# Entry of the second layer in a two-layer Mamba-2/MLA step: the last row square and the scaling of the third row group moved behind columns of the first group, gate weight remainders computed in four parts

## Chip, cores and metric

The kernel runs on one core of a Trainium2 chip. The metric is the device time in microseconds (us) of one execution. The profile is of one execution on the same kind of core.

## What is computed

One inference step of a two-layer decoder trunk. Layer 0 is a Mamba-2 mixer, layer 1 multi-head latent attention (MLA) with a gate. There are 1024 prompt tokens and 64 sample tokens (8 requests of 8), 1088 rows of width 1024, all in fp32. The part that matters here, cut from the reference, is the seam between the two layers:

```python
hp = hp + out_p                        # residual rows after layer 0 (hs likewise)
ln = rms_norm(hp, norm_w[1])           # x * rsqrt(mean(x*x) + 1e-6) * w
proj = einsum('btd,de->bte', ln, w_in) # layer 1: 512 query, 256 latent, 32 rope, 1024 gate columns
gate = proj[..., o3:]                  # later: o * silu(gate)
```

## The kernel before

**Precision.** Matmuls run on rounded fp32 operands. Each operand is held as two tiles, a rounded `h` part and the remainder `l` = x - h, and a product is three matmuls: h*h, l*h, h*l. So the normalised, transposed activations are `hh` and `hl`, and a weight block has `wgh` and `wgl` (gate) or `ck0h`/`ck0l` and so on (latent and rope columns). `split` (L127) makes such a pair: ACT copies to `h`, and another engine subtracts for `l`; for the gate and latent weights that is POOL (`eng=k.nc.gpsimd`).

**End of layer 0.** `ssd_out` (L792) finishes the residual rows in 9 tiles: rows 0 to 7 of 128 tokens, row 8 of 64. For each row and each half of 512 columns, PE makes a projection `pob` in PSUM and DVE adds it to the residual row `xrb` (L808). Row 8 needs a second add per half (L810), since its products lie in two halves of the PSUM tile. Then the row goes to DRAM (L815; rows 7 and 8 by POOL's queue), ACT squares it with a running sum (L818), DVE and POOL make of the sum the row's factor `hrs` (`rstd_of`, L202 and L207), and for rows 0 to 5 DVE multiplies the row by it at once (`scale_row`, L213) into `xt`.

**Entry of layer 1.** `norm_steps(..., tail=True)` (L258, called from `mla_in` at L967) takes the rows in three groups: rows 0 to 2, 3 to 5, 6 to 8 (384, 384 and 320 tokens). It first scales rows 6 to 8 (L260 to L262). Then `norm_cols` (L242) goes through the 8 column blocks of 128 of each group: PE transposes the block's three row pieces into a PSUM tile `xtp` (L248, three transposes), ACT writes `hh` of it (L250), DVE writes `hl` (L251). There are three `xtp` buffers, so the fourth block's transposes need the first block's `hl` done. I write T0,0 to T2,7 for the transposes by group and block.

After each group, `proj_piece` of the first two gate blocks (`gate_block`, L920) uses these columns: per block and gate three matmuls of 384 (or 320) columns, L88, into PSUM tiles `pj`. There are two `pj` buffers, which the projections `pob` of layer 0 used just before. A scheduler mixes all of this: each engine has one queue, run in order, and the scheduler chooses the order within it from the dependencies and its own estimates; `issue_after` holds an instruction behind a named one. A gate block ends with ACT's Silu out of PSUM (L925) and a DMA. Gate blocks 2 to 7 follow (`mla_in`, L972 to L980), then the latent, query and attention stages.

**Loads.** `load_w` (L283) puts each weight block's DMA on SP's queue (L285) into raw buffers, two for the gate blocks and two for the `ck` blocks. A third block's DMA therefore waits until POOL has made the first block's remainder, and SP's queue is in order too.

Of the kernel before, what the change touches and what calls it, by code (L numbers as in the profile page):

```python
# [8 lines left out]
F32 = mybir.dt.float32  # L9
# [7 lines left out]
D = 1024  # L17
# [106 lines left out]
    pass  # L124


def split(k, hi, lo, src, eng=None):  # L127
    nc = k.nc
    nc.scalar.copy(hi, src)  # L129
    (eng or nc.vector).tensor_tensor(lo, src, hi.bitcast(F32), op=ALU.subtract)  # L130


def setup(k, stack):
# [73 lines left out]
    nc.gpsimd.tensor_tensor(out, out, e, op=ALU.pow)  # L207


def scale_row(k, i, pool):  # L210
    xr, m = k.hr[i]
    xt = pool.tile([128, D], F32, tag="xt", name=f"xt{i}", bufs=3 if i > 5 else 6)
    k.nc.vector.tensor_scalar(xt[:m], xr[:m], k.hrs[:m, i : i + 1], None, op0=ALU.mult)  # L213
    return xt, m, 128 * (i % 3)
# [27 lines left out]
def norm_cols(k, gi, xs, wcol, hi, lo, psum):  # L242
    nc = k.nc
    t0, n = TG[gi]
    for d in range(8):
        p = psum.tile([128, 512], F32, tag="tr", name=f"xtp{gi}_{d}", bufs=PB["tr"])
        for xt, m, o in xs:
            nc.tensor.transpose(p[:, o : o + m], xt[:m, d * 128 : d * 128 + 128], k.ident[:m, :m])  # L248
        k.cols[gi].append(
            nc.scalar.activation(hi[:, d, t0 : t0 + n], p[:, :n], AF.Copy, scale=wcol[:, d : d + 1]))  # L250
        nc.vector.scalar_tensor_tensor(  # L251
            lo[:, d, t0 : t0 + n], p[:, :n], wcol[:, d : d + 1], hi[:, d, t0 : t0 + n].bitcast(F32),
            op0=ALU.mult, op1=ALU.subtract)
    if gi == 2:
        nc.gpsimd.tensor_copy(hi[:, :, T:], lo[:, :, SEQ:].bitcast(F32))


def norm_steps(k, load, wcol, hi, lo, pool, psum, steps, xbufs, before=None, after=None, tail=False):  # L258
    if tail:
        for i in range(6, 9):  # L260
            k.hrows.append(scale_row(k, i, pool))
    rows = k.hrows[:3] if tail else norm_rows(k, 0, load, pool, xbufs)  # L262
    if before is not None:
        before()
        wcol = k.normc[0]
    k.cols = [[], [], []]
    for gi in range(3):
        norm_cols(k, gi, rows, wcol, hi, lo, psum)
        if gi < 2:
            rows = k.hrows[3 * gi + 3 : 3 * gi + 6] if tail else norm_rows(k, gi + 1, load, pool, xbufs)  # L270
        if after is not None and gi == 0:
            after()
        for st in steps:
            next(st)


def load_raw(pool, nk, ncol, bufs=2):
# [2 lines left out]
    return t.rearrange("p (k e) -> p k e", k=nk)  # L280


def load_w(k, pool, src, nk, ncol, tag, bufs=3, raws=None, rbufs=2, eng=None):  # L283
    raw = load_raw(raws or pool, nk, ncol, rbufs)
    k.nc.sync.dma_start(raw, src.rearrange("(k p) e -> p k e", p=128))  # L285
    hi = pool.tile([128, nk, ncol], F32R, tag=tag + "h", name=tag + "h", bufs=bufs)
    lo = pool.tile([128, nk, ncol], F32R, tag=tag + "l", name=tag + "l", bufs=bufs)
    split(k, hi, lo, raw, eng)
    return hi, lo


# [501 lines left out]
def ssd_out(k, items, ypools, psum):  # L793
# [3 lines left out]
    for n, (ph, i) in enumerate(items):  # L797
# [3 lines left out]
        for hf in range(2):  # L801
# [9 lines left out]
            if hf == 0:  # L811
                if n + 1 < len(items):
                    nxt = items[n + 1][0].prep(items[n + 1][1], ypools[(n + 1) % 2], psum)
                yield
        (nc.gpsimd if ph.k0 and i > 6 else nc.sync).dma_start(k.h_d[t0 : t0 + m], xr[:m])  # L815
        if ph.k0:
            sq = k.tok.rearrange("p i a h -> p (i a h)")[:, :D]
            nc.scalar.activation(sq[:m], xr[:m], AF.Square, accum_out=k.hssq[:m, i : i + 1])  # L818
            rstd_of(k, k.hrs[:m, i : i + 1], k.hssq[:m, i : i + 1], D)
            k.hr.append((xr, m))  # L820
            if i < 6:
                k.hrows.append(scale_row(k, i, k.h0p))
        yield
# [94 lines left out]


def gate_block(k, wp, raws, b):  # L920
    ws = kslices(load_w(k, wp, k.I["mla_w_in"][0][:, 800 + 128 * b : 928 + 128 * b], 8, 128, "wg", 3, raws, eng=k.nc.gpsimd), 8)
    gt = wp.tile([128, T], F32, tag="gt", name=f"gt{b}", bufs=2)

    def ev(ci, t0, n, p):
# [1061 lines left out]
```

## Time and profile before

| | us |
|---|---|
| median of 3 runs | 1981.43 (1976.2, 1981.67, 1981.43) |
| the profiled execution, its own time | 1988.45 |
| its span, first to last instruction | 1986.7 |
| PE busy in the span | 1909.0 (96%) |
| DVE, ACT, POOL busy | 1204.0, 1110.3, 837.9 |
| 1054.61 to 1096.50 (entry of layer 1): length, PE busy, mean TensorE clock | 41.89, 37.31, 0.92 |
| 1096.50 to 1172.50 (gate blocks 2 to 7): the same | 76.00, 75.00, 1.00 |

How to read it. Times in the rows are from the span's start. A row of the timeline merges neighbours of one kind on one engine: start, length, engine, line, output <- input, shape, count, and in brackets how long the engine sat idle before and what ended that. A row of the windows view gives for a stretch the busy time of each engine with its count of instructions, then the clock granted to TensorE (1.00 is full), the mean busy share of the DMA engines, and GB/s. "PEld" is the weight load that goes along with each matmul. Buffer numbers are left out in the profile's names, and kept in the rows of order below.

### The profile page before, as it was taken

How to read it: one execution, taken by the hardware profiler on the slowest of the kernel's cores; microseconds unless marked ns; L12 is line 12 of the kernel's file. 1: busy time of each engine (PE TensorE's matmuls, PEld its weight loads, DVE VectorE, ACT ScalarE, POOL GpSimd, SP SyncE). 2: the span in 40 equal slices, each digit the busy share in tenths (PEclk: the TensorE clock that was granted, in tenths of full speed). 3: DMA queues.
4: the chain of work that ended last, by engine and by line, in shares of the span. 5: the costliest groups of instructions: out<-in, count | busy, mean ns of one | idle time of the engine just before them, and what ended most of it. 6: DMA issues, size and time to landing. Idle time of an engine off the chain costs nothing. (4 is left out here: it accounts for less than half of the span.)

```text
span 1986.7 us, 33396 instructions
## 1 busy us (share of the span) xinstructions
PE 1909.0 (96%) x12001; PEld 1738.7 (88%) x12001; DVE 1204.0 (61%) x2439; ACT 1110.3 (56%) x2535; POOL 837.9 (42%) x1018
## 2 busy tenths in 40 slices
PE   6999999999999999899999999998999999899998
PEld 5999999999999999788787998997888887688887
DVE  4557575756665656755434114566788787766665
ACT  5456666666666666633214224436777777645552
POOL 1537455555655555443003221204333335755541
PEclk9999999999999999999999999999999999899999
DMA  4223323332333332645433242222111113544441
GB/s 152 59 65 88 90 84 96 83 106 83 95 83 95 81 96 89 200 153 183 148 126 121 89 165 66 99 84 74 45 50 40 50 40 100 189 139 140 138 146 38
DMA packets 181228, 202.12 MB, mean 102 GB/s; under 512 B 18844, under 2 KB 147752, under 8 KB 180680
## 3 DMA queue, kind: packets, MB, share of 16 engines
q1 hardware_dynamic: 176008, 180.21, 29.9%
q0 software_dynamic: 4976, 19.66, 3.1%
q8 instruction: 95, 1.56, 0.3%
q14 instruction: 69, 0.57, 0.1%
q10 hardware_dynamic: 80, 0.13, 0.0%
HBM read 146.65 MB, written 53.28 MB: 101 GB/s over the span
## 5 line engine op out<-in xcount | busy, mean ns | idle before, releaser
L88 PE MATMUL pj<-xh,wih 128*128 128x384 f32 (+1 forms) x768 | 255.8, 337 | 5.0 <-ACT xh L250 4.4
L88 PE MATMUL pj<-xl,wih 128*128 128x384 f32 (+1 forms) x768 | 255.3, 332 | 0.6 <-DVE xl L251 0.6
L88 PE MATMUL pj<-xh,wil 128*128 128x384 f32 (+1 forms) x768 | 254.6, 332 | 0.0
L1344 POOL TENSOR_TENSOR tl<-P,th 128x384 fp32r<-128x384 f32 (+1 forms) x96 | 91.9, 957 | 160.8 <-ACT P L1342 119.2
L487 DVE SCALAR_TENSOR_TENSOR acc<-raw,vec,acc 128x1112 f32<-128x1112 f32 x96 | 141.6, 1476 | 25.8 <-ACT acc L483 24.9
L88 PEld LDWEIGHTS pj<-xh,wih 128*128 128x128 f32 x768 | 145.1, 190 | 6.8 <-ACT xh L250 5.1
L88 PEld LDWEIGHTS pj<-xl,wih 128*128 128x128 f32 x768 | 145.7, 190 | 1.9 <-DVE xl L251 0.9
L88 PEld LDWEIGHTS pj<-xh,wil 128*128 128x128 f32 x768 | 145.5, 189 | 0.4
L100 PE MATMUL pz<-wih,xh 128*128 128x256 f32 x504 | 142.8, 287 | 0.8 <-ACT z L528 0.8
L100 PE MATMUL pz<-wil,xh 128*128 128x256 f32 (+1 forms) x504 | 140.2, 284 | 0.0
L1341 ACT ACTIVATE th<-st 128x512 fp32r<-128x512 f32 x192 | 94.5, 492 | 75.7 <-PE st L1337 54.9
L591 ACT ACTIVATE M<-M,tok 128x128 f32<-128x128 f32 (+1 forms) x288 | 90.9, 386 | 68.6 <-DVE M L588 68.4
L100 PE MATMUL pz<-wih,xl 128*128 128x256 f32 x448 | 128.3, 286 | 0.0
L1633 POOL TENSOR_TENSOR kvl<-pgr,kvh 128x1024 fp32r<-128x1024 f32 x32 | 77.6, 2424 | 71.6 <-ACT kvh L1632 71.6
L100 PEld LDWEIGHTS pz<-wih,xh 128*128 128x128 f32 x504 | 96.0, 190 | 1.6 <-ACT z L528 1.2
L588 DVE TENSOR_TENSOR M<-M,negu 128x512 f32<-128x512 f32 x64 | 52.2, 815 | 69.0 <-DMA M<-acs_d 68.7
L1342 ACT ACTIVATE P<-st 128x512 f32<-128x512 f32 x192 | 93.4, 486 | 0.0
L100 PEld LDWEIGHTS pz<-wil,xh 128*128 128x128 f32 (+1 forms) x504 | 92.7, 184 | 0.7
L130 DVE TENSOR_TENSOR wil<-wraw,wih 128x512 fp32r<-128x512 f32 x88 | 71.2, 815 | 30.4 <-ACT wih L129 27.1
L1344 DVE TENSOR_TENSOR tl<-P,th 128x512 fp32r<-128x512 f32 x96 | 74.8, 779 | 21.8 <-ACT P L1342 21.3
L574 POOL TENSOR_TENSOR xdd<-xsT,tok 128x256 f32<-128x256 f32 x64 | 51.2, 800 | 81.3 <-ACT xsT L560 81.0
L100 PEld LDWEIGHTS pz<-wih,xl 128*128 128x128 f32 x448 | 85.3, 190 | 0.1
(827 smaller groups left out, 6343.5 us busy)
## 6 DMA issues: line engine op xcount, KB each, us to landing
wraw<-in_ssd_w_in SPq DMA_DIRECT2D x92, 256.0 KB
M<-acs_d SPq DMA_DIRECT2D x64, 256.0 KB
s<-in_state_ssm SPq DMA_DIRECT2D x32, 256.0 KB
y_d<-y SPq DMA_DIRECT2D x64, 128.0 KB
out_s_ssm<-s SPq DMA_DIRECT2D x32, 256.0 KB
wraw<-in_ssd_w_out SPq DMA_DIRECT2D x12, 512.0 KB
q_d<-qt SPq DMA_DIRECT2D x32, 192.0 KB
qp<-q_d SPq DMA_DIRECT2D x8, 768.0 KB
```

The lines of the kernel that those rows point to most:

```text
L88: nc.tensor.matmul(out, a, b, start=(i == 0), stop=(i == n - 1))
L100: nc.tensor.matmul(o, a, b, start=(j == 0), stop=(j == len(ops) - 1))
L130: (eng or nc.vector).tensor_tensor(lo, src, hi.bitcast(F32), op=ALU.subtract)
L487: last = nc.vector.scalar_tensor_tensor(acc, raw[:, j : j + n], k.convw[j][:, blk : blk + 1], acc, op0=ALU.mult, op1=ALU.add)
L574: nc.gpsimd.tensor_tensor(v3(xdd), v3(xsT), hb(2), op=ALU.mult)
L588: nc.vector.tensor_tensor(M[:m, :, :m], M[:m, :, :m], (k.negs if smp else k.negu)[:m, :m].unsqueeze(1).to_broadcast([m, 4, m]), op=ALU.add)
L591: nc.scalar.activation(M[:m, h, :m], M[:m, h, :m], AF.Exp, bias=tk[:, 0, 4 * g + h : 4 * g + h + 1])
L1341: nc.scalar.activation(th[:, :n], ps[:, :n], AF.Exp, scale=SCALE)
L1342: nc.scalar.activation(P[:, :n], ps[:, :n], AF.Exp, scale=SCALE)
L1344: eng.tensor_tensor(tl[:, :n], P[:, :n], th[:, :n].bitcast(F32), op=ALU.subtract)
L1633: nc.gpsimd.tensor_tensor(rl, raw, rh.bitcast(F32), op=ALU.subtract)
```

## The change

It has four parts. (1) The square of row 8 and its factor are taken out of `ssd_out` and put into `norm_steps` behind group 0, held by `issue_after` behind the ACT and DVE columns of block 2; the square's unneeded output goes to a new tile `hsq8` instead of `tok`. (2) The scaling of rows 6, 7 and 8 moves from ahead of group 0 to behind its `hl` columns 4, 5 and 6. (3) Row 8's DMA to DRAM is issued after the first step of the gate blocks, still by POOL, in program order. (4) The remainder of a gate weight block, one POOL instruction of 128x1024, becomes four of 128x256 (`parts=4`, all eight gate blocks). Nothing is left out of the computation.

```diff
-def split(k, hi, lo, src, eng=None):
+def split(k, hi, lo, src, eng=None, parts=0):
     nc = k.nc
     nc.scalar.copy(hi, src)
-    (eng or nc.vector).tensor_tensor(lo, src, hi.bitcast(F32), op=ALU.subtract)
+    n = parts and hi.shape[1] // parts
+    for a in range(parts):
+        s = slice(a * n, a * n + n)
+        (eng or nc.vector).tensor_tensor(lo[:, s], src[:, s], hi[:, s].bitcast(F32), op=ALU.subtract)
+    if not parts:
+        (eng or nc.vector).tensor_tensor(lo, src, hi.bitcast(F32), op=ALU.subtract)
...
+def square_row(k, i, junk):
+    xr, m = k.hr[i]
+    k.nc.scalar.activation(junk[:m], xr[:m], AF.Square, accum_out=k.hssq[:m, i : i + 1])
+    rstd_of(k, k.hrs[:m, i : i + 1], k.hssq[:m, i : i + 1], D)
...
 def norm_steps(k, load, wcol, hi, lo, pool, psum, steps, xbufs, before=None, after=None, tail=False):
-    if tail:
-        for i in range(6, 9):
-            k.hrows.append(scale_row(k, i, pool))
...
-    k.cols = [[], [], []]
+    k.cols, k.lows = [[], [], []], []
     for gi in range(3):
         norm_cols(k, gi, rows, wcol, hi, lo, psum)
+        if tail and gi == 0:
+            with k.tc.issue_after(k.cols[0][2].ins), k.tc.issue_after(k.lows[2].ins):
+                square_row(k, 8, pool.tile([128, D], F32, tag="sq", name="hsq8", bufs=1))
+            for i in range(6, 9):
+                with k.tc.issue_after(k.lows[i - 2].ins):
+                    k.hrows.append(scale_row(k, i, pool))
...
         for st in steps:
             next(st)
+        if tail and gi == 0:
+            xr, m = k.hr[8]
+            k.tc.keep_in_program_order(k.nc.gpsimd.dma_start(k.h_d[TILES[8][0] : T], xr[:m]))
...
-        (nc.gpsimd if ph.k0 and i > 6 else nc.sync).dma_start(k.h_d[t0 : t0 + m], xr[:m])
+        if i < 8 or not ph.k0:
+            (nc.gpsimd if ph.k0 and i > 6 else nc.sync).dma_start(k.h_d[t0 : t0 + m], xr[:m])
         if ph.k0:
-            sq = k.tok.rearrange("p i a h -> p (i a h)")[:, :D]
-            nc.scalar.activation(sq[:m], xr[:m], AF.Square, accum_out=k.hssq[:m, i : i + 1])
-            rstd_of(k, k.hrs[:m, i : i + 1], k.hssq[:m, i : i + 1], D)
             k.hr.append((xr, m))
+            if i < 8:
+                square_row(k, i, k.tok.rearrange("p i a h -> p (i a h)")[:, :D])
...
-    ws = kslices(load_w(k, wp, k.I["mla_w_in"][0][:, 800 + 128 * b : 928 + 128 * b], 8, 128, "wg", 3, raws, eng=k.nc.gpsimd), 8)
+    ws = kslices(load_w(k, wp, k.I["mla_w_in"][0][:, 800 + 128 * b : 928 + 128 * b], 8, 128, "wg", 3, raws, eng=k.nc.gpsimd, sub=4), 8)
```

What becomes of the order, on three engines. ACT at the end of layer 0, before; `xrb8` is row 8, `xtp0_0` to `xtp0_4` the transposed blocks of group 0, `wraw` a raw weight block:

```order
L129 CAST ck1h_13142<-wraw_13140 128x288
L818 ACTIVATE tok_72,hssq_1116<-xrb8_12337 64x1024
L250 ACTIVATE hh_12400<-xtp0_0_12417,vec_142 128x384
L250 ACTIVATE hh_12400<-xtp0_1_12423,vec_142 128x384
L250 ACTIVATE hh_12400<-xtp0_2_12429,vec_142 128x384
L250 ACTIVATE hh_12400<-xtp0_3_12435,vec_142 128x384
L129 CAST wgh_12768<-wraw_12766 128x1024
L250 ACTIVATE hh_12400<-xtp0_4_12441,vec_142 128x384
```

The same place on ACT in the changed kernel:

```order
L129 CAST ck1h_13161<-wraw_13159 128x288
L261 ACTIVATE hh_12396<-xtp0_0_12407,vec_142 128x384
L261 ACTIVATE hh_12396<-xtp0_1_12413,vec_142 128x384
L261 ACTIVATE hh_12396<-xtp0_2_12419,vec_142 128x384
L217 ACTIVATE hsq8_12455,hssq_1116<-xrb8_12337 64x1024
L261 ACTIVATE hh_12396<-xtp0_3_12425,vec_142 128x384
L261 ACTIVATE hh_12396<-xtp0_4_12431,vec_142 128x384
L129 CAST wgh_12775<-wraw_12773 128x1024
L261 ACTIVATE hh_12396<-xtp0_5_12437,vec_142 128x384
```

The square of row 8 went from ahead of the first `hh` column to behind the third, and the cast of the third gate block from behind column 3 to behind column 4. Further on, the casts `ck2h` to `ck7h` also stand later among the columns: `ck2h` and `ck3h` now behind column 7 of group 0, `ck4h` to `ck7h` behind columns 3 to 6 of group 1.

DVE from the last half of row 8 on, before (`pob81` is the projection's right half):

```order
L808 TENSOR_TENSOR xrb8_12337<-xrb8_12337,pob81_12358 64x512
L213 TENSOR_SCALAR xt6_12411<-xrb6_12183,hrs_1115 128x1024
L213 TENSOR_SCALAR xt7_12413<-xrb7_12260,hrs_1115 128x1024
L810 TENSOR_TENSOR xrb8_12337<-xrb8_12337,pob81_12358 64x512
L202 TENSOR_SCALAR hrs_1115<-hssq_1116 64x1
L251 SCALAR_TENSOR_TENSOR hl_12401<-xtp0_0_12417,vec_142,hh_12400 128x384
L251 SCALAR_TENSOR_TENSOR hl_12401<-xtp0_1_12423,vec_142,hh_12400 128x384
```

DVE from the same instruction on, in the changed kernel:

```order
L825 TENSOR_TENSOR xrb8_12337<-xrb8_12337,pob81_12358 64x512
L827 TENSOR_TENSOR xrb8_12337<-xrb8_12337,pob81_12358 64x512
L262 SCALAR_TENSOR_TENSOR hl_12397<-xtp0_0_12407,vec_142,hh_12396 128x384
L262 SCALAR_TENSOR_TENSOR hl_12397<-xtp0_1_12413,vec_142,hh_12396 128x384
L262 SCALAR_TENSOR_TENSOR hl_12397<-xtp0_2_12419,vec_142,hh_12396 128x384
L207 TENSOR_SCALAR hrs_1115<-hssq_1116 64x1
L262 SCALAR_TENSOR_TENSOR hl_12397<-xtp0_3_12425,vec_142,hh_12396 128x384
L262 SCALAR_TENSOR_TENSOR hl_12397<-xtp0_4_12431,vec_142,hh_12396 128x384
L224 TENSOR_SCALAR xt6_12459<-xrb6_12183,hrs_1115 128x1024
L262 SCALAR_TENSOR_TENSOR hl_12397<-xtp0_5_12437,vec_142,hh_12396 128x384
L224 TENSOR_SCALAR xt7_12461<-xrb7_12260,hrs_1115 128x1024
L262 SCALAR_TENSOR_TENSOR hl_12397<-xtp0_6_12443,vec_142,hh_12396 128x384
```

The two scalings left the gap between row 8's last two adds, and now stand one by one between the `hl` columns 4, 5 and 6; that of row 8 (`xt8`) stands behind column 6.

PE from the third block's last transpose on, in the changed kernel, with the engines that each instruction waits for; rows and waits are the same before but for line numbers:

```order
L259 MATMUL xtp0_2_12419<-ident_58,xt2_11944 128x128
L88 MATMUL pj_12475<-hh_12396,wgh_12467 128x384 [waits DVE_49,Activation_49]
L88 MATMUL pj_12511<-hh_12396,wgh_12503 128x384
L259 MATMUL xtp0_3_12425<-ident_58,xt0_11786 128x128 [waits DVE_49]
L259 MATMUL xtp0_3_12425<-ident_58,xt1_11865 128x128
L259 MATMUL xtp0_3_12425<-ident_58,xt2_11944 128x128
L88 MATMUL pj_12475<-hl_12397,wgh_12467 128x384
L88 MATMUL pj_12475<-hh_12396,wgl_12468 128x384 [waits Pool_49]
```

The first `pj` matmul waits for ACT's first `hh` column and for DVE's last add of row 8, which reads the `pj` buffer for the last time as `pob81`; T0,3 waits for the first `hl`. Further on in groups 0 and 1, PE's order differs in a few neighbouring matmuls.

On POOL, row 8's DMA now stands ahead of `ck0l` instead of behind it, and each `wgl` row is four rows of 128x256. SP's queue keeps its order. Outside this stage one neighbouring pair each on ACT and DVE changes places, in the sample attention.

8 lines of the change are left out of this document (4 added, 4 removed).

## The prediction

> **What bounds the kernel now.** I read the page's busy times first, then the chain of waits of the stretch 1020 to 1110 us, where the changed lines run, then the timelines of its engines, then windows for the clock.
>
> ```profile
> PE 1909.0 (96%) x12001; PEld 1738.7 (88%) x12001; DVE 1204.0 (61%) x2439; ACT 1110.3 (56%) x2535; POOL 837.9 (42%) x1018
> ```
>
> PE is busy 96% of the span. A change on ACT, DVE or POOL is worth the PE idle time or the PE clock that it gives back. So I look at where PE stands in the changed stage:
>
> ```profile
> 1054.61 1.14 PE L248 MATMUL xtp<-ident,xt 128*128 128x128 f32 x9
> 1059.49 1.01 PE L88 MATMUL pj<-hh,wgh 128*128 128x384 f32 x2 [3.73 <-ACT hh L250]
> 1060.30 0.84 PE L248 MATMUL xtp<-ident,xt 128*128 128x128 f32 x3
> ...
> 1072.99 0.82 PE L248 MATMUL xtp<-ident,xt 128*128 128x128 f32 x6
> ```
>
> PE makes the first nine transposes (T0,0 to T0,2) by 1055.75, then stands 3.73 us until the first `hh` column, and then works on. The third row starts T0,3, the last T1,2. What held ACT:
>
> ```profile
> 1052.39 0.43 ACT L129 CAST ck1h<-wraw 128x288 fp32r<-128x288 f32 x1
> 1057.62 1.06 ACT L818 ACTIVATE tok<-xrb 64x1024 f32<-64x1024 f32 x1 [4.81 <-issue]
> 1058.59 0.19 ACT L818 ACTIVATION_READ_ACCUMULATOR tok<-xrb 64x1 f32 x1
> 1058.86 1.53 ACT L250 ACTIVATE hh<-xtp,vec 128x384 fp32r<-128x384 f32 x3
> ```
>
> ACT idles 4.81 us ahead of row 8's square, with the transposes ready for most of it, and begins the columns only when the square is read out (1.24 us from 1057.62). The square waits for row 8's last add on DVE:
>
> ```profile
> 1051.14 0.68 DVE L808 TENSOR_TENSOR xrb<-xrb,pob 64x512 f32<-64x512 f32 x1 [1.59 <-PE pob L100]
> 1051.85 0.69 DVE L810 TENSOR_TENSOR xrb<-xrb,pob 64x512 f32<-64x512 f32 x1
> ...
> 1054.81 0.68 DVE L808 TENSOR_TENSOR xrb<-xrb,pob 64x512 f32<-64x512 f32 x1 [2.27 <-PE pob L100]
> 1055.42 1.40 DVE L213 TENSOR_SCALAR xt<-xrb,hrs 128x1024 f32<-128x1024 f32 x2
> 1056.85 0.69 DVE L810 TENSOR_TENSOR xrb<-xrb,pob 64x512 f32<-64x512 f32 x1
> 1059.47 1.67 DVE L251 SCALAR_TENSOR_TENSOR hl<-xtp,vec,hh 128x384 fp32r<-128x384 f32 x3 [0.52 <-ACT hh L250]
> ```
>
> Two scalings (1.40 us) stand between row 8's adds, which elsewhere follow each other in 0.71 us. The idle has a second price. These windows all have edges on one grid of 3.413 us, on which every change of the clock in this trace falls:
>
> ```profile
> 1055.15:1058.56 3.41, 0.60 (x6) 0.37 (x4) 2.36 (x4) 0.94 (x1) 3.01 (x3) 1.00 0.84 234
> 1058.56:1061.97 3.41, 2.48 (x9) 2.33 (x10) 1.99 (x5) 2.54 (x7) 1.25 (x2) 0.50 0.56 161
> 1061.97:1065.39 3.42, 3.42 (x13) 3.25 (x12) 2.12 (x3) 1.62 (x3) 2.62 (x2) 0.50 0.00 0
> 1065.39:1068.80 3.41, 3.41 (x24) 3.33 (x23) 1.54 (x3) 1.59 (x4) 1.77 (x2) 1.00 0.70 195
> ...
> 1352.15:1355.56 3.41, 2.06 (x10) 1.49 (x9) 2.20 (x8) 0.58 (x1) 3.35 (x5) 1.00 0.03 4
> 1355.56:1358.97 3.41, 1.92 (x13) 1.31 (x11) 3.31 (x8) 2.96 (x6) 3.33 (x4) 0.99 0.00 0
> 1358.97:1362.38 3.41, 2.80 (x8) 2.31 (x9) 1.62 (x4) 2.49 (x5) 2.64 (x3) 0.50 0.02 7
> 1669.56:1672.97 3.41, 1.81 (x9) 1.27 (x9) 1.46 (x4) 2.19 (x4) 1.16 (x1) 1.00 0.24 61
> 1672.97:1676.38 3.41, 3.41 (x13) 3.02 (x13) 1.91 (x6) 1.26 (x4) 1.00 (x1) 0.50 0.00 0
> ```
>
> A window with PE busy 1.92 us or less is followed by half clock (0.50), one with 2.06 us is not. The stage lost its clock from 1058.56 to 1065.39.
>
> **The change, part by part.** *Square and scalings moved (the first two parts).* In the new order DVE makes row 8's last add straight behind the one at 1054.81: at 1055.52, by the 0.71 us above, done at 1056.21. ACT is free from 1052.8, so the first three `hh` need only their transposes: from about 1055.1, when a third of the nine is through, done about 1056.7 (1.53 us). PE's first two `pj` matmuls need that add too (they take over its PSUM buffer): start 1056.24 instead of 1059.49, 0.5 us of PE idle instead of 3.73. The first `hl` runs from 1056.21 to 1056.83 (one of the three in 1.67 us takes 0.62), and T0,3 needs it: the two matmuls end at 1056.75 (half of 1.01 us, at full clock), so T0,3 starts at 1056.88. That is **3.42 us** ahead of 1060.30; the idle falls from 3.73 to 0.62.
>
> From T0,3 to T1,2 PE had work without a break, 12.69 us (1060.30 to 1072.99), part of it at half clock. At full clock a block takes, by two rows of the chain of waits:
>
> ```profile
> 1078.99 0.33 PE xtp L248 x3
> 1079.32 1.05 PE pj L88 x6
> ```
>
> 1.38 us for three transposes and six matmuls, 0.175 a matmul. T0,3 to T1,2 is seven such blocks and four matmuls: 7 x 1.38 + 4 x 0.175 = 10.36 us, **2.33 us** less. An idle of 0.62 us leaves any window 2.79 us of work, above 2.06, so the clock stays. Sum: 3.42 + 2.33 = **5.75 us**.
>
> *What could take it back.* The square now costs ACT its 1.24 us behind the third `hh`: from 1056.6 to 1057.8. `hh` 3 follows and ends at 1058.4. PE reaches it after T0,3 to T0,5 and 16 matmuls (3 x 0.33 + 16 x 0.175 = 3.8 us), at 1060.7: covered by 2.3 us. The scalings put 0.70 us each (half of 1.40) between `hl` 4 to 7 on DVE. One may take longer:
>
> ```profile
> 1064.24 1.45 DVE L213 TENSOR_SCALAR xt<-xrb,hrs 64x1024 f32<-64x1024 f32 x1
> ...
> 1055.10 2.37 POOL L130 TENSOR_TENSOR ck0l<-wraw,ck0h 128x288 fp32r<-128x288 f32 x1
> 1058.49 0.80 POOL L130 TENSOR_TENSOR ck1l<-wraw,ck1h 128x288 fp32r<-128x288 f32 x1
> 1062.77 2.38 POOL L130 TENSOR_TENSOR wgl<-wraw,wgh 128x1024 fp32r<-128x1024 f32 x1 [2.95 <-ACT wgh L129]
> ```
>
> The 64-row scaling took 1.45 us and ended 0.54 us behind the `wgl` that ran beside it (1065.15); `ck0l`, beside the other two, took 2.37 us where its twin took 0.80. So these two kinds exclude each other, instruction by instruction. A scaling can then wait for one POOL part. By the same count T0,4 ends at 1058.4 and T0,5 at 1060.1; with 0.58 us for `hh` and 0.62 for `hl` behind each, `hl` 4 ends at 1059.7, before the third `wgl` can start, and the first scaling goes at once. `hl` 5 ends about 1061.4; with a wait of one part each, `hl` 6 ends about 1063.0 and `hl` 7 about 1064.4. PE needs them 8.3 and 9.7 us behind 1056.88 (6 blocks' transposes and 36 matmuls, 7 and 42), at 1065.2 and 1066.5. Covered by 2 us; if that cover were gone, each us of DVE would be one of PE.
>
> *The quarters.* A part of 128x256 takes between 0.60 us (a quarter of 2.38) and 0.80 (the 128x288 row); between the 288 and the 1024 row a straight line gives 0.73, which I take, as 288 is near. Four parts cost 2.9 us instead of 2.4, so 0.5 more a block (0 to 0.8), 4 us over eight blocks, on POOL. The first two blocks then end at 1056.2 (1050.38 + 8 x 0.73; at most 1056.8); PE's first use of the second one's remainder is at 1058.7. Later blocks:
>
> ```profile
> 1111.88 2.40 POOL L130 TENSOR_TENSOR wgl<-wraw,wgh 128x1024 fp32r<-128x1024 f32 x1 [9.93 <-ACT wgh L129]
> ```
>
> POOL sits idle 9.93 us ahead of this one: the cover. PE cost: 0.
>
> *Row 8's DMA and the loads.* POOL issues that DMA (0.6 us) ahead of `ck0l`; it waits for the add at 1056.21, just when POOL gets there. Nothing reads it here. SP's queue passes nothing, but its loads wait for POOL: the third gate block's DMA goes out 0.5 us later. The tight one is `ck6`, whose raw buffer is free after `ck4l`.
>
> ```profile
> 1066.38 0.33 SPq L285 DMA_DIRECT2D wraw<-in_mla_w_in  x1
> ...
> 1069.66 0.43 ACT L129 CAST ck4h<-wraw 128x288 fp32r<-128x288 f32 x1 [0.38 <-DMA wraw<-in_mla_w_in]
> ...
> 1074.04 0.87 ACT L925 ACTIVATE gt<-pj 128x384 f32<-128x384 f32 x2
> 1077.98 0.58 ACT L250 ACTIVATE hh<-xtp,vec 128x384 fp32r<-128x384 f32 x1 [0.99 <-PE xtp L248]
> ...
> 1082.79 0.62 PE L88 MATMUL pj<-hh,wgh 128*128 128x384 f32 x2
> ```
>
> Such a load took 3.28 us from issue to its cast. The `gt` pair, `hh` 1,5 and the matmuls behind T2,0 (last three rows) all move up by 5.75 us. Then two columns and `ck4h` follow `gt`, so `ck4h` starts at 1070.0, `ck4l` ends at 1071.3, and `ck6` is there at 1074.6. ACT gets to `ck6h` behind `hh` 1,5, at 1072.8, and waits 1.8 us with `hh` 1,6 behind it (0.43 + 0.58 us), which is done by 1075.6. PE first needs that column at 1077.0, behind T2,0. Covered by 1.4 us.
>
> From T1,2 on PE has the same work and waits as before, so I carry the 5.75 us to the end. Against the profiled execution: 1988.45 - 5.75 = 1982.7 us. That execution lies 7.0 us above the median of the runs shown; the forecast against the median is 1981.43 - 5.8 = **1975.6 us**.
>
> **The rivals.** *B: the clock was not ours to win.* If only a wholly idle window trips, the gap does so in 0.32 of 3.41 placements (3.73 less 3.41), the profiled execution was a rare one, and a usual one wins the idle alone, 3.73 - 0.62 = 3.1 us: 1978.3. Against it stand the windows above: any placement of 3.73 us leaves some window at least 1.87 us idle, so 1.54 or less busy, where 1.92 was enough to trip.
> [...]
>
> *C: a later stretch goes too.* Two later windows, the one at 1669.56 with 1.81 us and
>
> ```profile
> 1690.05:1693.46 3.41, 1.90 (x8) 1.05 (x7) 3.32 (x6) 1.87 (x5) 0.72 (x2) 1.00 0.00 0
> ```
>
> this one, tripped by a little. The program moves by 5.75 us, which is 1.7 windows, so the grid cuts those gaps elsewhere. A stretch of 6.83 us at half clock costs 3.0 us (the chain shows 2.51 us for 8 matmuls at half, 1.05 for 6 at full: 44% lost): 1981.43 - 5.75 - 3.0 = 1972.7. The mirror, the 2.06 window of 1352.15 tripping, gives 1978.7; it counts with B.
>
> ```profile
> 1063.06 2.51 PE pj L88 x8
> ```
>
> *D: slower than before.* ACT stands at `ck6h` until its load lands. Each us beyond 1076.0 stops PE; beyond 1.5 us the window trips, 3.0 us more. At 1078.7, that is 7.4 us from issue, 2.75 + 3.0 eats the gain; at 9.4 us it is 1983.4, at 13.4 us 1987.4. The 3.28 us above speaks against it.
>
> *E: the change does not do it.* Something else holds the first column, time 1981.4. The order shows nothing else there.
>
> **How the numbers follow.** A, the forecast, 52%. Its idle term is 3.1 us; its clock term, 2.65 here, runs with the grid's place from 1.5 (one window, 3.41 x 0.44) to 3.0 us (two): 1975.3 to 1976.8. C 24%, B with its mirror 12%, E 6%, D 6%. A measurement can tell 0.3% from no change, 5.94 us, so 1975.49. A lies on that edge, and the runs of before differ by 5.5 us among themselves, so half of A counts as faster. Faster: 24 + 26 = 50%. Slower by as much: half of D, 3%. Within: 47%. The range takes A, B, C and two stretches moving instead of one on the fast side, and leaves out E and D: 1971 to 1979.5.
>
> **What would show it.** Right: the first `pj` matmul about 0.5 us behind the transposes, ACT's square behind three `hh` columns, TensorE at 1.00 throughout the entry, T1,2 5.75 us earlier from T0,0. Wrong: an idle above 1.35 us in a window of the entry, `hl` 5 to 7 behind PE, `ck6h` holding `hh` 1,6 beyond T2,0, or the gain given back behind 1172 us, where the clock's stretches have moved.

## The result, and the profile after

The changed kernel took 1971.86 us (median of 8 runs, 1967.28 to 1977.47), the kernel before 1978.18 us beside it (8 runs, 1976.2 to 1981.67). The ratio is 0.9962, with an interval of 0.9948 to 0.9975: 7.5 us less, between 4.9 and 10.3. Two further comparisons of the same two kernels gave 0.9976 (0.9962 to 0.9991) and 0.9966 (0.9952 to 0.9979), so 4.8 and 6.7 us. The forecast was 5.75 us off the profiled execution and 1975.6 us against the median of three runs. The profiled execution of after took 1970.05 us, span 1967.9.

Engines of after, busy us and share of the span:

```profile
PE 1898.9 (96%) x12001; PEld 1730.7 (88%) x12001; DVE 1198.9 (61%) x2439; ACT 1110.0 (56%) x2535; POOL 840.3 (43%) x1042
```

PE lost 10.1 us of busy time with the same 12001 instructions: 13 windows of 3.41 us were at half clock in before, ahead of its end, and 5 in after, and in before 8 `pj` matmuls took 2.51 us at half clock (0.31 each), 6 at full clock 1.05 (0.175 each). The extra 24 POOL instructions are the gate parts.

PE of after at the entry (start, duration, instruction, count; in brackets the idle ahead and what ended it):

```profile
1049.68 1.15 PE L259 MATMUL xtp<-ident,xt 128*128 128x128 f32 x9
1051.43 0.59 PE L88 MATMUL pj<-hh,wgh 128*128 128x384 f32 x2 [0.60 <-ACT hh L261]
...
1062.38 0.82 PE L259 MATMUL xtp<-ident,xt 128*128 128x128 f32 x6
1063.97 0.44 PE L88 MATMUL pj<-hh,wgh 128*128 128x384 f32 x1 [0.77 <-ACT gt L942]
...
1086.98 0.44 PE L88 MATMUL pj<-hh,wgh 128*128 128x384 f32 x1 [1.17 <-ACT gt L942]
```

The idle ahead of the first `pj` matmuls is 0.60 us (0.62 forecast, 3.73 before). From T0,0 to T1,2 it is 12.70 us, before 18.38: 5.68 us less, where 5.75 was forecast. I call the **entry** the stretch from T0,0 to the last row here, the second wait of PE for `gt`: 37.30 us. In before that row is

```profile
1097.50 0.44 PE L88 MATMUL pj<-hh,wgh 128*128 128x384 f32 x1 [1.08 <-ACT gt L925]
```

and the entry 42.89 us, so 5.6 us are still there at its end. ACT of after:

```profile
1050.29 1.52 ACT L261 ACTIVATE hh<-xtp,vec 128x384 fp32r<-128x384 f32 x3 [2.40 <-PE xtp L259]
1051.70 1.05 ACT L217 ACTIVATE hsq<-xrb 64x1024 f32<-64x1024 f32 x1
...
1052.74 0.57 ACT L261 ACTIVATE hh<-xtp,vec 128x384 fp32r<-128x384 f32 x1
...
1068.58 0.43 ACT L129 CAST ck6h<-wraw 128x288 fp32r<-128x288 f32 x1 [0.62 <-DMA wraw<-in_mla_w_in]
1068.91 0.58 ACT L261 ACTIVATE hh<-xtp,vec 128x384 fp32r<-128x384 f32 x1
```

The first three columns now follow the transposes, and the square stands behind the third, as the order had it. ACT waits 0.62 us for the load of `ck6`, where I had worked out 1.8. DVE of after:

```profile
1049.88 0.68 DVE L825 TENSOR_TENSOR xrb<-xrb,pob 64x512 f32<-64x512 f32 x1 [2.27 <-PE pob L100]
1050.60 0.69 DVE L827 TENSOR_TENSOR xrb<-xrb,pob 64x512 f32<-64x512 f32 x1
1051.32 1.67 DVE L262 SCALAR_TENSOR_TENSOR hl<-xtp,vec,hh 128x384 fp32r<-128x384 f32 x3
...
1054.76 0.75 DVE L224 TENSOR_SCALAR xt<-xrb,hrs 128x1024 f32<-128x1024 f32 x1
...
1057.87 1.31 DVE L224 TENSOR_SCALAR xt<-xrb,hrs 64x1024 f32<-64x1024 f32 x1
```

Row 8's adds follow each other in 0.72 us, and the scalings run between the `hl` columns; the last still takes 1.31 us beside POOL, and no row of PE waits for it. POOL's gate parts of the first two blocks:

```profile
1045.45 5.59 POOL L133 TENSOR_TENSOR wgl<-wraw,wgh 128x256 fp32r<-128x256 f32 x8 [0.18 <-ACT wgh L129]
```

A part is 0.70 us (0.73 forecast). Last the clock of after in the windows of the entry (edges, length, busy us of PE, PEld, DVE, ACT, POOL, granted TensorE clock, DMA share and GB/s):

```profile
1049.84:1053.25 3.41, 2.81 (x21) 2.27 (x19) 3.09 (x6) 2.96 (x6) 2.83 (x5) 1.00 0.71 198
1053.25:1056.67 3.42, 3.42 (x24) 3.35 (x23) 2.62 (x5) 2.16 (x4) 2.53 (x4) 1.00 0.74 254
```

The clock stays at 1.00 throughout (1.00 too over the whole stretch from 1049.68 to 1086.98). So the entry does what was forecast. What has to be explained is the rest: the spans of the two profiled executions lie 18.8 us apart (1986.7 against 1967.9), and only 5.6 of these are the entry. 4.9 us lie ahead of T0,0 (1054.61 against 1049.68), 8.3 us behind the entry.

### The profile page after: what moved, and what is told of

Same layout as the page of the kernel before. It is cut to its first block, busy times and chain, and to the rows that moved or that the text cites. A ratio compares the mean times of both kernels' runs of the same rounds, so it can differ in the third digit from the quotient of the medians.

```text
span 1967.9 us, 33423 instructions
## 1 busy us (share of the span) xinstructions
PE 1898.9 (96%) x12001; PEld 1730.7 (88%) x12001; DVE 1198.9 (61%) x2439; ACT 1110.0 (56%) x2535; POOL 840.3 (43%) x1042
## 4 chain that ended last, share of the span: by engine, by line
PE 71%; POOL 6%; DMA 6%; ACT 5%; DVE 5%; issue 5%; SPq 0%; POOLq 0%; DVEq 0%; ACTq 0%
PE pj L88 18%; PE pz L100 8%; PE pq L100 6%; PE pob L100 5%; PE poa L100 5%; PE py L613 2%; PE st L1347 2%; POOL kvl L1650 2%; PE o L1378 2%; DMA M<-acs_d 2%; PE sc L1315 2%; PE o L1380 2%; PE st L1348 2%; PE st L1349 2%; PE o L1379 2%
```

## The experiments

The table gives each time by its ratio to the kernel before, run beside it, and the stages of its profiled execution: the entry, from there to the transposes `nkp`, to the `o40n` matmuls of the sample attention, and to the first `act` transposes there.

| kernel | ratio (95%) | us by the ratio | entry | to `nkp` | to `o40n` | to `act` |
|---|---|---|---|---|---|---|
| before | 1 | | 42.89 | 557.74 | 37.92 | 46.98 |
| after | 0.9962 (0.9948 to 0.9975) | -7.5 | 37.30 | 555.31 | 34.02 | 45.68 |
| whole_again | 0.9976 (0.9962 to 0.9991) | -4.8 | 37.31 | 555.78 | 34.16 | 45.49 |
| whole_third | 0.9966 (0.9952 to 0.9979) | -6.7 | 37.31 | 556.25 | 34.13 | 44.89 |
| moves_only | 0.9983 (0.9969 to 0.9998) | -3.4 | 37.25 | 556.45 | 37.84 | 46.93 |
| moves_again | 0.9970 (0.9956 to 0.9983) | -5.9 | 37.29 | 554.61 | 34.14 | 45.28 |
| quarters_only | 0.9999 (0.9987 to 1.0012) | -0.2 | 43.07 | 553.30 | 36.44 | 45.46 |
| scalings_only | 0.9981 (0.9967 to 0.9996) | -3.8 | 40.15 | 556.38 | 37.68 | 45.04 |
| square_only | 0.9979 (0.9966 to 0.9993) | -4.2 | 40.17 | 556.27 | 33.63 | 45.33 |
| warm_gap | 1.0018 (1.0008 to 1.0028) | +3.6 | 42.17 | 562.60 | 33.98 | 45.62 |
| warm_late_casts | 1.0007 (0.9993 to 1.0021) | +1.4 | 40.52 | 561.98 | 38.21 | 46.53 |
| late_casts | 0.9990 (0.9978 to 1.0002) | -2.0 | 42.82 | 554.07 | 38.13 | 46.79 |
| stt_scale | 0.9972 (0.9963 to 0.9981) | -5.5 | 37.31 | 556.11 | 36.63 | 45.39 |
| act_scale | 1.0010 (0.9999 to 1.0021) | +2.0 | 37.29 | 553.55 | 34.74 | 42.60 |
| act_scale_first | 0.9974 (0.9960 to 0.9987) | -5.1 | 37.31 | 555.61 | 34.55 | 43.49 |

The theory: two waits were cut (ACT's square, DVE's scalings between the adds), and with them an idle of 3.1 us and a half-clock stretch of 2.3 to 2.65 us; the four parts do nothing. The rivals: B, the clock was not won by the idle; C, later stretches went too; and that the parts, which also change POOL, had a share.

### Which part of the change does it

**moves_only**: the change without the four parts.

```diff
-..., raws, eng=k.nc.gpsimd, sub=4), 8)
+..., raws, eng=k.nc.gpsimd), 8)
```

> The change without the four parts: a gate remainder is one POOL instruction again; square, scalings and row 8's DMA stay moved. Theory A (idle and clock of the entry): the whole gain, 5.0 to 8.0 us below the kernel before, first pj matmul 0.5 to 0.7 us behind the nine transposes, T0,0 to T1,2 within 0.3 us of 12.70, TensorE at 1.00 from T0,0 to T1,2. Rival Q (the parts carry what is above 5.8): 1 to 2 us less gain than the changed kernel. Rival B (idle alone): 3.1 us.

**quarters_only**: before, with the four parts alone (`parts` in `split`, `sub=4` for the gate blocks).

> The kernel before with only the four parts (eight gate blocks, 128x256 each). Theory A: no change, within 1.5 us of the kernel before, the gap of about 3.7 us in front of the first pj stays, with half clock behind it, and T0,0 to T1,2 stays at 16.5 to 18.5 us. Rival Q: 1.5 us or more faster, or a shorter gap. Rival for the other side (the 0.4 to 0.5 us that a block of parts costs more shows on PE): up to 4 us slower.

**scalings_only**: before, with the scalings of rows 6 to 8 moved and the square left.

```diff
-    if tail:
-        for i in range(6, 9):
-            k.hrows.append(scale_row(k, i, pool))
...
+        if tail and gi == 0:
+            for i in range(6, 9):
+                with k.tc.issue_after(k.lows[i - 2].ins):
+                    k.hrows.append(scale_row(k, i, pool))
```

> The kernel before with only the scalings of rows 6, 7 and 8 moved behind hl 4, 5 and 6; the square of row 8 stays ahead of the first hh. Row 8's last add then ends 1.33 us earlier, ACT's 1.24 us of square still stand ahead of hh 0: PE idle about 2.25 us instead of 3.73, T0,3 1.6 us earlier. Theory A: a gap of 2.25 us leaves a window with less than 2.0 us of work in most placements on the grid, so the clock is mostly still lost: gain 1.0 to 2.5 us, and half clock in the entry in the profile. Rival (the clock needs a wholly idle window, or nothing but idle counts): gain 1.6 us with the clock at 1.00. Rival additive (each half brings half of the whole): 3 to 4 us.

**square_only**: moves_only, with the scalings of rows 6 and 7 left ahead of group 0.

```diff
+    if tail:
+        for i in range(6, 8):
+            k.hrows.append(scale_row(k, i, pool))
...
-            for i in range(6, 9):
+            for i in range(8, 9):
```

> The kernel before with the square of row 8 behind the third hh, its DMA and its scaling (which needs the square) behind; rows 6 and 7 are still scaled between row 8's two last adds. ACT is free, but row 8's last add ends at the old place, 1.8 us behind the transposes, and the first pj takes over its PSUM buffer: PE idle about 1.8 us, T0,3 about 2.1 us earlier than before. Theory A: the clock is lost in some 7 of 10 placements: gain 1.5 to 3.5 us. Rival (ACT's square alone was the wait): idle 0.6 us and the whole gain of 5.7 us. Rival (the last add alone was the wait): no gain, gap 3.7 us.

The parts alone keep the idle at 3.73 us and the time at 0.9999 of before. Moving alone has the entry of the whole (37.25). PE of quarters_only, of moves_only, of scalings_only and of square_only, each from T0,0 on:

```profile
1052.38 1.15 PE L253 MATMUL xtp<-ident,xt 128*128 128x128 f32 x9
1057.25 1.01 PE L88 MATMUL pj<-hh,wgh 128*128 128x384 f32 x2 [3.73 <-ACT hh L255]
```

```profile
1051.13 1.14 PE L259 MATMUL xtp<-ident,xt 128*128 128x128 f32 x9
1052.89 0.59 PE L88 MATMUL pj<-hh,wgh 128*128 128x384 f32 x2 [0.61 <-ACT hh L261]
```

```profile
1056.34 1.15 PE L259 MATMUL xtp<-ident,xt 128*128 128x128 f32 x9
1059.89 0.62 PE L88 MATMUL pj<-hh,wgh 128*128 128x384 f32 x2 [2.41 <-ACT hh L261]
1073.57 0.44 PE L88 MATMUL pj<-hh,wgh 128*128 128x384 f32 x1 [1.77 <-ACT gt L937]
```

```profile
1054.21 1.14 PE L259 MATMUL xtp<-ident,xt 128*128 128x128 f32 x9
1057.28 0.58 PE L88 MATMUL pj<-hh,wgh 128*128 128x384 f32 x2 [1.93 <-DVE xrb L830]
```

The releasers in brackets tell the two waits apart. With the scalings moved, DVE is through with row 8 early, but ACT still squares ahead of its columns: PE waits 2.41 us for `hh`. With the square moved, the columns are ready, and PE waits 1.93 us for DVE's add, behind two scalings. Each half brings the entry 2.7 us, and both together 5.6. It happens that the halves add up, but they do it from unlike terms: scalings_only wins 1.32 us of idle and the whole stretch, and loses 1.0 us to a longer wait for `gt` (1.77 against 0.77 us; just ahead of `gt`, ACT had stood 0.76 and 0.27 us for the loads of `ck4` and `ck5`); square_only wins 1.80 us of idle and one window of two. The windows, of scalings_only and of square_only:

```profile
1055.80:1059.22 3.42, 1.68 (x13) 1.23 (x10) 1.39 (x3) 1.15 (x2) 0.95 (x2) 1.00 0.55 147
1059.22:1062.63 3.41, 2.71 (x17) 2.32 (x18) 2.41 (x5) 3.03 (x6) 3.41 (x3) 1.00 0.43 83
```

```profile
1054.54:1057.95 3.41, 1.48 (x11) 0.98 (x10) 3.35 (x6) 2.30 (x4) 3.03 (x3) 1.00 0.85 242
1057.95:1061.37 3.42, 3.42 (x14) 3.23 (x15) 1.68 (x5) 2.47 (x5) 2.56 (x4) 0.50 0.55 170
```

PE was busy 1.48 us in a window of square_only, and half clock followed; it was busy 1.68 us in one of scalings_only, and none did, although I had expected half clock there too. My bounds of 1.92 and 2.06 us for this are therefore wrong.

### Once more: the whole and the moves

The first times of after and moves_only differed (-7.5 and -3.4 us), although their entries agree to 0.05 us. Both were run again beside each other, the whole a third time later.

> The changed kernel again, to size its gain beside the kernel with only the moves on one chip. Theory A (the whole gain is idle and clock of the entry): 4.5 to 7 us below the kernel before, 5.7 the likeliest, 9 nines of the entry as in the first profile (T0,0 to the idle at the end of the second gate block 37.3 us against 42.9). Rival Q (the four parts add 2 to 4 us once the moves are there): 7 to 9 us below the kernel before again, and 2 us or more below the moves alone.

> Square, scalings and row 8's DMA moved, the gate remainders in one POOL instruction each: the first comparison gave 3.4 us below the kernel before, the entry in its profile was the changed kernel's to 0.1 us. Theory A: that was spread, so 4 to 7 us below the kernel before now, within 2 us of the changed kernel beside it. Rival Q: 2 to 4 us again, 2 us or more above the changed kernel.

> The changed kernel a third time, for the size of its gain. So far 7.5 us (4.9 to 10.3) and 4.8 us (1.8 to 7.5) below the kernel before. Theory A, 5.7 us of entry: 4 to 7.5 us here too, and the mean of the three within 1 us of 5.7. Rival (something besides the entry gains 1.5 us or more): a mean of 7.2 us or more.

The order turned round: the whole 4.8 us, the moves 5.9, each inside the other's interval, with medians of 1973.92 and 1973.91 us; the third comparison gave 6.7. So the four parts have no effect that these runs can tell, and -7.5 and -3.4 were the spread. What spreads is outside the entry. In the table, all eight profiles with both moves have 37.25 to 37.31 us there, while the stretch to `o40n` is 34.0 to 37.8 us for the same instructions. The clock is the cause that the traces show: over all fifteen profiles, those without a half-clock window in that stretch took 33.6 to 34.7 us for it, the one with one window 36.4, those with two 36.6 to 38.2. At half clock outside the entry, and ahead of the end, were: in before 229.1 to 232.5 (one window), and two windows each from 1358.95, 1672.95, 1693.45, 1720.75 and 1737.8; in after one window each from 1340.0, 1350.2, 1677.9, 1701.8 and 1722.25. One such place in the sample attention, of before and of after:

```profile
1693.44:1696.85 3.41, 3.41 (x9) 2.21 (x9) 1.67 (x4) 1.23 (x4) 3.17 (x3) 0.50 0.19 41
1696.85:1700.27 3.42, 3.42 (x14) 3.13 (x13) 2.01 (x1) 1.56 (x3) 3.04 (x3) 0.50 0.73 225
1700.27:1703.68 3.41, 3.41 (x23) 3.00 (x22) 2.49 (x5) 2.50 (x6) 1.02 (x1) 1.00 0.24 44
```

```profile
1674.48:1677.89 3.41, 2.22 (x10) 1.30 (x9) 3.28 (x6) 1.21 (x3) 1.90 (x2) 1.00 0.00 0
1677.89:1681.30 3.41, 3.41 (x13) 2.82 (x12) 1.36 (x3) 2.74 (x7) 3.24 (x4) 0.50 0.32 67
1681.30:1684.72 3.42, 3.42 (x24) 3.15 (x23) 3.42 (x3) 2.50 (x6) 3.21 (x2) 1.00 0.81 242
```

In before the clock stays down for a second window, though PE was fully busy in the first; in after it comes back behind one. Why, the runs don't show. The timed runs point the same way: over 112 runs of the kernel before, beside these kernels, the longer runs had the lower mean granted clock, with a correlation of -0.63 (-0.26 to -0.83 in the four sets of comparisons taken singly) and 1.3 us for 0.001 of clock. So the clock is part of the spread; that it is all of it is not shown. Six runs at 0.987 and 0.988 took 1985.0 us on average, four at 0.994 and 0.995 took 1974.9. The whole had a mean clock 0.0008 (whole_again) and 0.0020 (whole_third) above before's; the entry's stretch alone, 6.83 us at half of 1980, is 0.0017.

### The clock by itself

By the theory, the clock stays if PE has other work during the idle, although the first column is as late as before. **warm_gap** is before with 22 transposes into unused PSUM columns behind T0,2; the cast of the third gate block is held behind the fourth column (`xtp0_3`), where it stands in before; the changed kernel has it one column later. The transposes are extra work that nothing reads.

```diff
+        for _ in range(warm if d == 2 else 0):
+            nc.tensor.transpose(p[:, 384:], xs[0][0][:, :128], k.ident)
...
+    k.hold = k.cols[0][3] if b == 2 else None
```

> The kernel before with 22 more transposes of row 0's first block behind T0,2, into 128 unused columns of that PSUM tile; nothing reads them. The cast of the third gate block is held behind the fourth hh, as it stood before. They fill some 2.4 us of the 3.73 us for which PE waits, so that the wait stays and the clock is not lost. Theory A: first pj at the old place behind T0,2 (3.6 to 3.9 us), 0.9 to 1.5 us of it idle, TensorE at 1.00 through the entry, T0,0 to the end of the second gate block 39.8 to 40.8 us (42.9 less 2.65): gain 1.5 to 3.5 us. Rival B (the clock was not there to be won in a usual run): within 1 us of the kernel before. Rival for the other side (what is reordered by the longer PE queue costs): slower.

The idle was 1.33 us and the clock 1.00, but the entry took 42.17 us, not some 40.5. ACT of warm_gap:

```profile
1063.91 0.58 ACT L253 ACTIVATE hh<-xtp,vec 128x384 fp32r<-128x384 f32 x1 [0.80 <-PE xtp L249]
1067.88 0.44 ACT L130 CAST ck4h<-wraw 128x288 fp32r<-128x288 f32 x1 [3.38 <-DMA wraw<-in_mla_w_in]
1068.21 0.58 ACT L253 ACTIVATE hh<-xtp,vec 128x384 fp32r<-128x384 f32 x1
```

This is rival D's mechanism at another load: PE, faster now, needs the first column of group 1 earlier, ACT stands 3.38 us at `ck4h`, and that column (the third row) is queued behind it. In the changed kernel the casts `ck2h` to `ck7h` come later in ACT's order. **warm_late_casts** holds them at those places, and **late_casts** is the same without the transposes.

```diff
+    late = {2: (0, 7), 3: (0, 7), 4: (1, 3), 5: (1, 4), 6: (1, 5), 7: (1, 6)} if tag == "ck" else {}
+    for kk in range(8):
+        k.hold = k.cols[late[kk][0]][late[kk][1]] if kk in late else None
```

> The kernel with the 22 added transposes once more, with the casts ck2h to ck7h held where the changed kernel has them (ck2h and ck3h behind column 7 of group 0, ck4h to ck7h behind columns 3 to 6 of group 1). In warm_gap the clock stayed at 1.00, but ACT stood 3.38 us for the load of ck4 with the first hh of group 1 behind it, since PE and ACT got there earlier and the load did not. Theory A with that wait: T0,0 to the end of the second gate block 40.2 us (39.8 to 40.6) instead of 42.17, the wait ahead of ck4h at most 1 us and covered. Total 1.5 to 3.5 us below the kernel before, if the entry alone counts; if it is above the kernel before again, as warm_gap was by 3.6 us, the rest lies behind the entry. Rival (the wait at ck4h was not the cause): 42 us again.

> The kernel before with nothing but those casts held late on ACT; no added transposes, square and scalings as before. Theory A: no change, the entry 42.6 to 43.2 us with 3.7 us idle and half clock, total within 1.5 us of the kernel before. Rival (the later casts, which came with the change as a side effect, carry part of its gain by themselves): 1 us or more faster.

With late casts the warm entry took 40.52 us; without the transposes it is 42.82, idle 3.73, and two windows at half clock (1053.62 to 1060.44) as before. PE of warm_late_casts, the window of its wait, and PE of late_casts:

```profile
1057.01 1.15 PE L249 MATMUL xtp<-ident,xt 128*128 128x128 f32 x9
1057.99 2.56 PE L251 MATMUL xtp<-ident,xt 128*128 128x128 f32 x22
1061.89 0.62 PE L88 MATMUL pj<-hh,wgh 128*128 128x384 f32 x2 [1.33 <-ACT hh L253]
```

```profile
1059.53:1062.95 3.42, 2.06 (x16) 1.49 (x15) 1.64 (x5) 2.68 (x5) 2.30 (x4) 1.00 0.90 253
```

```profile
1054.82 1.01 PE L88 MATMUL pj<-hh,wgh 128*128 128x384 f32 x2 [3.73 <-ACT hh L253]
```

The first `pj` matmuls start 4.88 us behind T0,0 in both, exactly as in before. So the 2.3 us are the clock's alone, as forecast (2.33), and rival B falls: the gap left no window wholly idle, and yet it took the clock in all three profiles that have it whole (before, quarters_only, late_casts), while filling it kept the clock in both that fill it. That it was kept was luck in part: the windows of the wait held only 2.05 and 2.06 us of work, and some windows with as much are followed by half clock (see the threshold below). The late casts do nothing by themselves (0.9990 with 1 inside), but in the warm kernel without them most of the gain of the clock is lost at the loads.

Neither warm kernel is faster as a whole, although I had expected 1.5 to 3.5 us of both. Behind the entry both need 562 us to `nkp` instead of 553 to 558. Part of that is a load that landed late; PE of warm_gap there:

```profile
1466.55 0.50 PE L1335 MATMUL st<-qTh,kTh 98*128 98x512 f32 x1 [2.00 <-ACT P L1347]
```

In its profile SP issues that `w_uk` load at 1460.40 and ACT's cast starts at 1465.41, 5.0 us behind. This happened to three of the last six such loads in the two kernels' profiles (each has four, and the first is left out). It cost PE 2.0 to 2.07 us each time, and a half-clock window followed two of the three; in the thirteen other profiles these loads took 2.7 to 2.8 us. What makes them late is not settled, nor whether the timed runs had them late too, so the whole time of the warm kernels stays open.

### The next wait: the sample attention

The largest idle of PE left behind the entry is 4.1 us ahead of the first `act` transposes. DVE of after there, and POOL of after beside it:

```profile
1717.17 0.47 DVE L1698 SCALAR_TENSOR_TENSOR ac<-ac,f,o 128x256 f32<-128x256 f32 x1
1717.68 4.17 DVE L1701 TENSOR_SCALAR ac<-ac,ln 128x256 f32<-128x256 f32 x1
```

```profile
1717.02 2.37 POOL L1826 TENSOR_TENSOR w5l<-w5r,w5h 128x1024 fp32r<-128x1024 f32 x1
1719.34 2.34 POOL L1650 TENSOR_TENSOR kvl<-pgr,kvh 128x1024 fp32r<-128x1024 f32 x1
```

A scaling of 128x256 takes 4.17 us here, where the median of the eight in after is 0.34, and ends 0.17 us behind the second of two POOL subtractions (1721.85 against 1721.68). I tried to take it away from that in three ways, on top of the change. **stt_scale** writes it as a `scalar_tensor_tensor`:

```diff
-            nc.vector.tensor_scalar(st[2], st[2], ln, None, op0=ALU.mult)
+            nc.vector.scalar_tensor_tensor(st[2], st[2], ln, st[2], op0=ALU.mult, op1=ALU.bypass)
```

> The changed kernel with one form of instruction changed in the sample attention: the last scaling of the 128x256 sum is a scalar_tensor_tensor (its second operation passes the product on) instead of a tensor_scalar. In both profiles the first of these tensor_scalars took 4.2 to 4.5 us beside a POOL subtraction, and PE stood 4.1 to 4.4 us for it. If these two kinds exclude each other as the row scaling and POOL's remainders did: 0.5 us for that instruction, PE's idle ahead of the act transposes 0.5 to 1.5 us, the half clock behind it gone in most runs, 3 to 7 us below the changed kernel. If it waits for something else, or the new form is excluded too: 4 us as before, no change.

DVE of stt_scale, and POOL of stt_scale beside it:

```profile
1727.18 4.62 DVE L1701 SCALAR_TENSOR_TENSOR ac<-ac,ln 128x256 f32<-128x256 f32 x1
```

```profile
1726.84 2.37 POOL L1826 TENSOR_TENSOR w5l<-w5r,w5h 128x1024 fp32r<-128x1024 f32 x1
1729.16 2.34 POOL L1650 TENSOR_TENSOR kvl<-pgr,kvh 128x1024 fp32r<-128x1024 f32 x1
```

My theory, that only the `tensor_scalar` form is shut out, falls: the new form took 4.62 us. The `scalar_tensor_tensor` of after at 1717.17, of the same shape but with `o` in PSUM, took 0.47 us, although POOL's subtraction had begun 0.15 us ahead of it. So the form alone does not decide. What differs between the two are the operands (both inputs of the new one are in SBUF), but no run changed their place alone, so that it decides is not shown. The new one also ended behind a second subtraction (1731.80 against 1731.50), which had started 1.98 us behind it.

**act_scale** puts the scaling on ACT, in all eight places; **act_scale_first** in the first only.

```diff
-            nc.vector.tensor_scalar(st[2], st[2], ln, None, op0=ALU.mult)
+            nc.scalar.activation(st[2], st[2], AF.Copy, scale=ln)
```

> The changed kernel with the last scaling of the 128x256 sums in the sample attention on ACT instead of DVE (eight of them). On DVE the first one took 4.2 to 4.6 us in both forms tried, until two POOL subtractions beside it were through, and PE stood 4.1 to 4.5 us. If it was shut out by POOL: 0.4 us on ACT behind the casts that stand ahead of it, the act transposes 1.5 to 3 us earlier, and a half-clock stretch less in part of the runs: 2 to 5 us below the changed kernel, 8 to 11 us below the kernel before. If PE then waits as long for the accT copy or the next cast: no change, 5 to 6 us below the kernel before.

> The changed kernel with only the first of the eight last scalings on ACT, the seven later ones on DVE as before. With all eight on ACT the stage from o40n to the act transposes took 42.6 us instead of 45.5, but each of six later ones held PE 0.92 us, and from the first act transposes to the last pt it took 200.7 us instead of 193.1. If both follow: 42.4 to 42.9 us for the first stage, 193 to 194 for the second, PE's wait ahead of the act transposes 2.1 us instead of 4.1 to 4.5, and 2 to 4 us below the changed kernel, 8 to 10 us below the kernel before. If what is saved ahead of the transposes is lost right behind them: the second stage 195 us or more and no gain over the changed kernel.

PE of act_scale, and of act_scale_first:

```profile
1722.46 0.44 PE L1708 MATMUL act<-ident,ac 128*128 128x128 f32 x2 [2.13 <-ACT ac L1701]
...
1757.42 0.44 PE L1708 MATMUL act<-ident,ac 128*128 128x128 f32 x2 [0.92 <-ACT ac L1701]
```

```profile
1725.09 0.44 PE L1711 MATMUL act<-ident,ac 128*128 128x128 f32 x2 [2.14 <-ACT ac L1702]
1730.77 0.50 PE L100 MATMUL p<-w5l,oh 128*128 128x512 f32 x1 [1.31 <-DVE w5l L1829]
```

On ACT the first wait falls to 2.13 us. But ACT has casts queued ahead of the scaling, and at six of the later places it is the later engine: 0.92 us each. Behind two of these waits (at 1856.92 and 1925.13) a window at half clock follows as well. From the first `act` transposes to the last `pt` transposes that PE waits for it is 200.7 us instead of 193.1, and against the kernel before nothing is left of what the change had won (1.0010). With only the first on ACT, the wait is 2.14 us and a new one of 1.31 us appears 5.7 us behind it, on DVE: the next DVE instruction there (`ol`, 128x1024) took 4.83 us instead of 1.21. Its 1973.78 us stand against 1972.65 us of the whole beside it. No version beats the changed kernel.

## Why the prediction was right, and where it was not

- **What bounds the kernel: right.** PE's idle and clock in the entry were the price; the two waits that carried it were read rightly, and each half by itself leaves the other wait (2.41 us for `hh`, 1.93 us for the add).
- **Idle, 3.73 to 0.62: right** (0.60). **Clock, 2.33 us: right**, shown alone by warm_late_casts against late_casts (42.82 - 40.52 = 2.3). **Sum, 5.75 us: right**, 5.68 at T1,2 and 5.6 at the end of the entry, in every kernel with both moves.
- **The threshold: wrong in its numbers**, without an effect here. I put it between 1.92 and 2.06 us of PE work in a window. All fifteen profiles, read on their grids from the twentieth us on, show half clock behind every window of 1.48 us or less, behind some between 1.49 and 2.23 (1.49 without it in after, from 824.55; 2.23 with it in act_scale_first, from 1702.78), and never from 2.24 on. The profile of before itself had a window that speaks against my bounds, and I had not read it; the window behind it is at 1.00:

```profile
826.45:829.86 3.41, 1.86 (x10) 1.17 (x8) 3.35 (x4) 2.72 (x7) 2.54 (x3) 1.00 0.66 200
```

The entry's window has 2.81, the old one 0.60, so the outcome was the same.

- **The covers: right.** Square, scalings and parts (0.70 us each) cost PE nothing that shows. The wait at `ck6h` was 0.62 us, not 1.8, and did not reach PE. The scalings and POOL's parts delayed each other in after as in before: the second and third scaling took 0.86 and 1.31 us and ended 0.54 and 0.55 us behind the end of a part (1056.80 and 1058.63), and the part ahead of the last took 1.19 us instead of 0.70. But the third was still running when two parts had ended (1057.94 and 1058.63), where I had counted a wait of one. The mechanism of D is real, though: in warm_gap ACT stood 3.38 us at `ck4h`. I named the late casts in the order, but gave them no part in the prediction. In the warm kernels they are what keeps the gain (40.52 us with them, 42.17 without); the changed kernel was not run without them, so what they are worth there is not shown.
- **Rivals.** B is refuted: the window of square_only that was followed by half clock held 1.48 us of PE work. C, a later stretch that goes too, is what the first pair of profiles looks like, but those stretches come and go between runs of one kernel; no lasting effect is shown. One stretch is at half clock ahead of `o40n` in two of the eight profiles with both moves and in five of the seven others, which is too few to tell. E is refuted.
- **The step that failed is "How the numbers follow"**, with the sentence that leads to it, "so I carry the 5.75 us to the end": the mechanism was right, and the carrying to a time was not. Two terms of that sum were off. The first is the baseline. The median of three, 1981.43 us, was 3.25 us too high: eight runs of the same kernel had 1978.18, later sets 1978.46 to 1981.52 in the median, single runs 1972 to 1989. I took the spread of those three runs, 5.5 us, for the edge of a verdict, but not for an error of the number that I subtracted from. The second is what happens behind the entry, which I put at nothing because the work is the same. The work is the same, but the time is not: half-clock windows come and go there, and the two profiled executions lie 8.3 us apart behind the entry. So 1975.6 was missed by 3.7 us, 3.25 of them the baseline and 0.5 the gain (6.3 us between the two medians). The first ratio gave a gain of 7.5 us, 1.75 above the forecast, and the chances had put 5.75 just short of the 5.94 us that a measurement can tell. That 1971.86 still lies in the range is partly luck: its low end was made for rival C, not for a wrong baseline.
- **How large the gain is.** The three comparisons of the whole gave 7.5, 4.8 and 6.7 us, 6.3 on average, 0.6 above the forecast. With the two of the moves alone, which have the same entry, the average is 5.7 us (3.4 to 7.5), which is what the entry gives (5.6). Whether the whole wins more than its entry, the runs can't tell.

## What to carry to other kernels

Where PE is busy 96% of the time, look for its idles of 2 us and more and price each twice, as idle and as the clock windows behind it; here the second price was 2.3 of 5.6 us. When the engine that first releases PE has been helped, ask which other wait of the same instruction ends next, and which loads the faster engine will now be too early for: half of the change was worth half, and in warm_gap, without the later casts, most of the clock's gain was gone again within 20 us (0.7 of 2.3 us left). A forecast of 0.3% needs the spread of the baseline in its range, and a comparison side by side.

## What the runs showed of the hardware

- In the fifteen profiles TensorE fell to half clock behind windows of 3.413 us (187 of them from 1055.15 to 1693.46 in before) with little PE work, and they were not all idle: behind 1.48 us and less always, behind 1.49 to 2.23 us sometimes, behind 2.24 us and more never. Where PE was busy for all 3.41 us of the first window at half clock, the clock came back behind that one in after (1677.89) and behind a second in before (1693.44); by the matmul rates of the prediction (8 in 2.51 us at half clock, 6 in 1.05 us at full) a stretch costs an estimated 1.5 us for one window and 3 us for two. The 112 runs of one kernel took 1972 to 1989 us, and the longer ones tended to have the lower mean clock (correlation -0.63).
- In the sample attention, the scaling of 128x256 on DVE, started beside a POOL subtraction, ended 0.17 to 0.30 us behind the second of two in a row: 4.17 us in after, 4.62 in stt_scale, where it had another form, against a median of 0.34 us in after. With it on ACT (act_scale_first), the next DVE instruction, of 128x1024, took 4.83 us instead of 1.21. What holds these instructions is not shown.
- POOL's subtraction took 0.70 us for 128x256, 0.80 for 128x288 and 2.37 for 128x1024: four parts cost 2.8 us. Beside DVE's scalings, as in quarters_only, eight of them took 7.02 us instead of 5.59.
